# One subtraction of token_sums is issued on GpSimd in place of VectorE

## The chip, the cores and the metric

The kernel runs on one core of a Trainium2 chip. The core has five engines with their own instruction queues: TensorE (PE, matrix products; its weight loads are listed as PEld), VectorE (DVE), ScalarE (ACT), GpSimd (POOL) and SyncE (SP, which here only starts transfers). Each queue runs in order, and an instruction that must wait for another engine holds up all that stands behind it in its own queue. The metric is the device time of one execution, in microseconds; less is better.

## The reference

The kernel computes one layer of a two-stream block: a mixer with recurrent heads (up to about 1075 us of the profile, and not touched here) and then a SwiGLU channel mixer with a 3x3 depthwise convolution, in float32. What the change touches is the channel mixer's up-projection of 512 tokens of width 2048 to twice 5504 columns:

```python
def conv_ffn(h, rows, cols, w_up, conv_w, conv_b, w_down):
    u = jnp.einsum('btd,df->btf', h, w_up)
    u_gate, u_val = jnp.split(u, 2, axis=-1)
    g = lax.conv_general_dilated(u_gate.reshape(b, rows, cols, D_FF), conv_w[:, :, None, :], ...)
    g = g.reshape(b, t, D_FF) + conv_b
    return jnp.einsum('btf,fd->btd', jax.nn.silu(g) * u_val, w_down)
```

## The kernel before

**Products.** Tokens lie along the free dimension, and the 2048 channels of `h2` are 16 tiles of 128 partitions, `x2[0]` to `x2[15]` (128x512 each; the profile calls them all x). Float32 accuracy comes from three products (`mm3`): both operands are split into a high part (`hi`, a cast on ACT) and a low part (`lo`, the rest, a subtraction on DVE), and high*high, high*low and low*high are accumulated. `split` is line 105 (ACT) and line 106 (DVE), every matmul is line 111.

**Groups.** The 43 blocks of hidden columns go in one group of three and ten groups of four (`QUADS`). The first group is multiplied plainly: `up_gate(0)` (tiles named ug) and then the value half (uv), each over eight pairs of channel tiles, `kp` 0 to 7. For each pair a weight tile is loaded (raw_uv, 128x768), split into hi_uv and lo_uv, and used by 18 matmuls. The weight pools for raw hold four buffers, those for hi and lo two each, so the split of pair k waits until PE is done with pair k-2.

**Products in seven.** From the second group on, a 2x2 block product is made from seven products in place of eight (`seven`, combined again by `four`). It needs sums and differences of weight quarters (`load_sums`) and of token quarters. The token part is made once, by `token_sums(j)` for j = 7 down to 0, and used by all groups from `up_gate(1)` on. A pair j has the tiles k0 = 2j and k1 = 2j+1, each with two halves of 256 tokens, written here (k0,0), (k0,1), (k1,0), (k1,1). After two biased copies on ACT (line 1217) it does:

- first subtraction: (k0,0) = (k0,1) - (k0,0)
- second subtraction: (k0,1) = (k0,1) - (k1,1), line 1219
- third subtraction: (k1,1) = (k1,1) - (k0,0)
- split of the whole of k0 into bth (ACT) and btl (DVE), 128x512
- fourth subtraction, into a tile that is free by then (`rest`), and the split of (k1,1), 128x256

The helper `sub` is line 94, so all four subtractions are DVE rows of line 94 in the profile before. `token_last` later splits `rest` into bqh and bql. Bth, btl, bqh and bql are first read when `up_gate(1)` starts.

**Order.** The code above is recorded in program order, but each engine's final order is chosen by a scheduler, which has its own idea of how long each instruction takes; `high_priority` and `issue_after` steer it. So a change in one line can move other instructions of the same queues. In the stage concerned DVE and ACT interleave four kinds of work: the splits of the weight pairs (lo_ug, lo_uv), the token sums, the taps of the 3x3 convolution of group 0 (`convolve`, line 1295, tiles cv), and the weight sums and splits of the next unit (sum_ug, lo_aug, lo_bug).

Of the kernel before, what the change touches and what calls it, by code (L numbers as in the profile page):

```python
# [15 lines left out]
ALU = mybir.AluOpType  # L16
# [67 lines left out]
def block_kernel(ctx: ExitStack, tc: tile.TileContext, a: dict, out: bass.AP):  # L84
    nc = tc.nc
    V, S, G, PE = nc.vector, nc.scalar, nc.gpsimd, nc.tensor
# [6 lines left out]
    def sub(o, x, y):  # L93
        V.tensor_tensor(out=o, in0=x, in1=y, op=ALU.subtract)  # L94
# [9 lines left out]
    def split(hi, lo, x):  # L104
        cast[0] = S.copy(hi, x).ins  # L105
        return V.tensor_tensor(out=lo, in0=x, in1=hi.bitcast(F32), op=ALU.subtract).ins  # L106
# [1085 lines left out]
    def flat(x):  # L1192
        return x.rearrange("p a b -> p (a b)")
# [12 lines left out]
    def half(k, i):  # L1206
        return x2[k][:, HW * i : HW * i + HW]

    def rest(j):

        return half(4 * (j // 2) + 2, j % 2)

    def token_sums(j):

        k0, k1 = 2 * j, 2 * j + 1
        for k in (k0, k1):
            S.activation(x2[k], x2[k], AF.Identity, bias=modc[3][:, k : k + 1])
        sub(half(k0, 0), half(k0, 1), half(k0, 0))
        sub(half(k0, 1), half(k0, 1), half(k1, 1))
        sub(half(k1, 1), half(k1, 1), half(k0, 0))  # L1220
        split(flat(bt[0][j][:, 0:2, :]), flat(bt[1][j][:, 0:2, :]), x2[k0])
        sub(rest(j), half(k1, 1), half(k1, 0))
        split(bt[0][j][:, 2, :], bt[1][j][:, 2, :], half(k1, 1))
# [130 lines left out]
    for j in reversed(range(KP)):  # L1354
        token_sums(j)
# [185 lines left out]
```

## Time and profile before

| quantity | value |
|---|---|
| median of 3 runs | 2442.56 us (2441.49 to 2443.43) |
| the profiled execution's own time | 2441.44 us |
| span in it, first to last instruction | 2439.7 us |
| mean granted TensorE clock | 0.998 |
| GpSimd busy over the span | 175.9 us (7%), 221 instructions |

The profiled execution lies 1.12 us under the median, inside the spread of the three runs; 1.74 us of its time lie outside the span. Times in rows of the profile are microseconds from the start of the span. In the rows of the timeline the first number is the start, the second the length, and what stands in brackets is idle time of that engine just before and who ended it. The stage concerned lies between 1100 and 1182 us.

### The profile page before, as it was taken

Reading aid. Unit: us, or ns where it says so; the run is one execution under the profiler, and the core shown is the slowest. Engines: PE = TensorE matmul, PEld = TensorE weight load, DVE = VectorE, ACT = ScalarE, POOL = GpSimd, SP = SyncE. Lnnn points to the kernel's source line nnn. Section 1 sums busy time; section 2 is a strip of 40 time slices with the busy share of each in tenths; the row PEclk is TensorE's granted clock in tenths of the full one; section 3 lists DMA queues with packets and bytes.
Section 4 is the critical chain, followed back from the end, with each engine's and each line's share of the span. In section 5 each row is a group of like instructions: output and inputs, shape, how many; then the busy total and the mean of one; then the engine's idle time right before and its main releaser. Section 6 shows DMA issues by size and latency. Waiting matters only on the chain.

```text
span 2439.7 us, 38673 instructions
## 1 busy us (share of the span) xinstructions
PE 2412.9 (99%) x15434; PEld 2173.7 (89%) x15434; DVE 1793.3 (74%) x2872; ACT 1005.2 (41%) x1498; POOL 175.9 (7%) x221
## 2 busy tenths in 40 slices
PE   8999999999999999999999999999999999999998
PEld 6888999899988888888898989899999999999997
DVE  6666856555456586779987887878787878787886
ACT  4225533322233232256544454445444444444445
POOL 0000000000000000000201010101011111111021
PEclk9999999999999999999999999999999999999999
DMA  9751111233455798833646464555555555546464
GB/s 388 284 173 56 46 53 44 78 121 114 137 189 191 237 321 275 287 130 109 145 132 154 116 151 123 137 134 141 136 130 139 134 143 122 146 123 154 113 185 135
DMA packets 122487, 373.67 MB, mean 153 GB/s; under 512 B 13912, under 2 KB 19010, under 8 KB 122306
## 3 DMA queue, kind: packets, MB, share of 16 engines
q1 hardware_dynamic: 95298, 318.75, 39.8%
q0 software_dynamic: 25920, 51.40, 11.7%
q8 instruction: 121, 1.98, 0.3%
q10 hardware_dynamic: 1088, 1.05, 0.1%
q14 instruction: 60, 0.49, 0.1%
HBM read 320.80 MB, written 50.34 MB: 152 GB/s over the span
## 4 chain that ended last, share of the span: by engine, by line
PE 94%; DVE 3%; DMA 1%; ACT 1%; issue 1%; SPq 0%; POOL 0%; POOLq 0%; ACTq 0%; DVEq 0%
PE a L111 19%; PE ug L111 18%; PE uv L111 18%; PE dn L111 18%; PE ga L111 7%; PE wo L111 7%; PE po L111 2%; PE ps_m L111 1%; PE sl L111 1%; PE st L111 1%; PE cst L111 1%; DMA raw_uv<-in_w_up 0%; DVE ex L94 0%; DMA xl<-in_xT 0%; DMA raw_m<-in_w_mod 0%
## 5 line engine op out<-in xcount | busy, mean ns | idle before, releaser
L111 PE MATMUL dn<-gh,lo_d 128*128 128x512 f32 x672 | 262.5, 391 | 2.3 <-DVE lo_d L106 2.3
L111 PE MATMUL dn<-gl,hi_d 128*128 128x512 f32 x672 | 261.6, 389 | 0.0
L111 PE MATMUL dn<-gh,hi_d 128*128 128x512 f32 x672 | 261.6, 389 | 0.0
L1295 DVE SCALAR_TENSOR_TENSOR cv<-pads,cwt,cv 128x512 f32<-128x512 f32 x344 | 239.2, 747 | 0.6
L1349 POOL DMA_DIRECT2D x2d<-st x160 | 140.1, 929 | 1142.0 <-ACT st L1348 1062.2
L106 DVE TENSOR_TENSOR lo_buv<-sum_uv,hi_buv 128x1024 fp32r<-128x1024 f32 x80 | 98.0, 1225 | 102.8 <-ACT hi_buv L105 102.7
L322 DVE SCALAR_TENSOR_TENSOR raw_m<-raw_m,crow 128x1024 f32<-128x1024 f32 x128 | 154.6, 1229 | 1.7 <-DMA raw_m<-in_w_mod 1.7
L111 PEld LDWEIGHTS dn<-gh,lo_d 128*128 128x128 f32 x672 | 126.1, 188 | 31.1 <-DVE lo_d L106 5.2
L111 PE MATMUL a<-hi_h,hTh 128*128 128x256 f32 x512 | 151.7, 296 | 0.5 <-ACT e L404 0.5
L111 PEld LDWEIGHTS dn<-gl,hi_d 128*128 128x128 f32 x672 | 126.2, 188 | 26.0
L111 PEld LDWEIGHTS dn<-gh,hi_d 128*128 128x128 f32 x672 | 126.2, 188 | 25.7
L111 PE MATMUL a<-lo_h,hTh 128*128 128x256 f32 x512 | 144.7, 283 | 0.0
L111 PE MATMUL a<-hi_h,hTl 128*128 128x256 f32 x512 | 144.6, 283 | 0.0
L105 ACT CAST hi_d<-raw_d 128x1024 fp32r<-128x1024 f32 x86 | 88.6, 1030 | 130.0 <-PE ug L111 70.3
L106 DVE TENSOR_TENSOR lo_d<-raw_d,hi_d 128x1024 fp32r<-128x1024 f32 x86 | 102.9, 1196 | 48.3 <-ACT hi_d L105 47.8
L111 PE MATMUL ug<-bth,hi_bug 128*128 128x256 f32 x480 | 136.8, 285 | 0.0
L111 PE MATMUL ug<-bqh,lo_aug 128*128 128x256 f32 x480 | 135.8, 283 | 0.0
L111 PE MATMUL uv<-bqh,lo_auv 128*128 128x256 f32 x480 | 135.8, 283 | 0.0
L111 PE MATMUL uv<-bth,hi_buv 128*128 128x256 f32 x480 | 135.8, 283 | 0.0
L111 PE MATMUL uv<-btl,hi_buv 128*128 128x256 f32 x480 | 135.8, 283 | 0.0
L111 PE MATMUL uv<-bth,lo_buv 128*128 128x256 f32 x480 | 135.8, 283 | 0.0
L111 PE MATMUL uv<-bql,hi_auv 128*128 128x256 f32 x480 | 135.8, 283 | 0.0
(414 smaller groups left out, 7262.7 us busy)
## 6 DMA issues: line engine op xcount, KB each, us to landing
raw_m<-in_w_mod SPq DMA_DIRECT2D x192, 512.0 KB, 5.1
raw_d<-in_w_down SPq DMA_DIRECT2D x82, 512.0 KB, 3.5
raw_ug<-in_w_up SPq DMA_DIRECT2D x80, 512.0 KB, 3.6
x2d<-st POOLq DMA_DIRECT2D x160, 256.0 KB, 5.6
raw_uv<-in_w_up SPq DMA_DIRECT2D x80, 512.0 KB, 5.4
raw_h<-in_w_heads SPq DMA_DIRECT2D x64, 512.0 KB, 3.6
raw_ga<-in_w_gates SPq DMA_DIRECT2D x32, 512.0 KB, 3.8
raw_wo<-in_w_out SPq DMA_DIRECT2D x32, 512.0 KB, 4.5
```

What stands on the lines that cost most here:

```text
L105: cast[0] = S.copy(hi, x).ins
L106: return V.tensor_tensor(out=lo, in0=x, in1=hi.bitcast(F32), op=ALU.subtract).ins
L111: ins = PE.matmul(*args, **kw)
L322: V.scalar_tensor_tensor(out=x, in0=x, scalar=1.0, in1=crow[0], op0=ALU.mult, op1=ALU.mult, accum_out=mtot[:, at : at + 1])
L1295: V.scalar_tensor_tensor(out=t3, in0=src, scalar=w, in1=t3, op0=ALU.mult, op1=ALU.add)
L1349: nc.gpsimd.dma_start(x2d[k], t, accum_op=ALU.add)
```

## The change

One line of `token_sums`: the second subtraction is issued on GpSimd (`G`) and not on VectorE. Its operands, its shape (128x256, float32, both inputs in SBUF) and its result are the same.

```diff
         sub(half(k0, 0), half(k0, 1), half(k0, 0))
-        sub(half(k0, 1), half(k0, 1), half(k1, 1))
+        G.tensor_tensor(out=half(k0, 1), in0=half(k0, 1), in1=half(k1, 1), op=ALU.subtract)
         sub(half(k1, 1), half(k1, 1), half(k0, 0))
         split(flat(bt[0][j][:, 0:2, :]), flat(bt[1][j][:, 0:2, :]), x2[k0])
```

The scheduler's result differs on DVE, ACT and POOL, and only between the first token subtraction and the first down-projection weight (lo_d_0); the rows of PE and of SP are the same. Three places follow, each a piece of the difference (- only before, + only in the change, no sign in both); x_12 is `x2[12]`, the last number is a buffer's.

DVE's queue, where the token sums of the pairs 6 and 7 (tiles 12 to 15) begin:

```order
 L94 TENSOR_TENSOR x_12_9113<-x_12_9113 128x256
 L94 TENSOR_TENSOR x_14_9117<-x_14_9117 128x256
-L94 TENSOR_TENSOR x_12_9113<-x_12_9113,x_13_9115 128x256
-L94 TENSOR_TENSOR x_14_9117<-x_14_9117,x_15_9119 128x256
+L94 TENSOR_TENSOR x_10_8810<-x_10_8810 128x256
 L94 TENSOR_TENSOR x_13_9115<-x_13_9115,x_12_9113 128x256
+L94 TENSOR_TENSOR x_15_9119<-x_15_9119,x_14_9117 128x256
 L106 TENSOR_TENSOR lo_ug_7_9473<-raw_ug_7_9470,hi_ug_7_9472 128x768
```

The second subtractions of the pairs 6 and 7 are gone from DVE; a first subtraction of pair 5 was pulled ahead, and the third subtractions of both pairs (into x_13 and x_15), which must wait for GpSimd now because it reads what they overwrite, stand ahead of the weight split lo_ug_7.

POOL's queue, between the stores of the residual stream and the first stores of the down-projection (line 1349):

```order
 L1171 DMA x2d_7894<-x_15_9119 128x512
+L1219 TENSOR_TENSOR x_12_9113<-x_12_9113,x_13_9115 128x256
+L1219 TENSOR_TENSOR x_14_9117<-x_14_9117,x_15_9119 128x256
+L1219 TENSOR_TENSOR x_10_8810<-x_10_8810,x_11_8812 128x256
+L1219 TENSOR_TENSOR x_8_8806<-x_8_8806,x_9_8808 128x256
+L1219 TENSOR_TENSOR x_6_8496<-x_6_8496,x_7_8498 128x256
+L1219 TENSOR_TENSOR x_4_8492<-x_4_8492,x_5_8494 128x256
+L1219 TENSOR_TENSOR x_2_8184<-x_2_8184,x_3_8186 128x256
+L1219 TENSOR_TENSOR x_0_8180<-x_0_8180,x_1_8182 128x256
 L1349 DMA x2d_7879<-st_0_10364 128x512
```

The eight subtractions stand there in one run; nothing else of POOL's work is passed.

DVE's queue around the weight splits lo_uv_3 and lo_uv_4:

```order
 L106 TENSOR_TENSOR bql_9222<-x_2_8184,bqh_9214 128x256
+L106 TENSOR_TENSOR lo_uv_3_9660<-raw_uv_3_9657,hi_uv_3_9659 128x768
+L106 TENSOR_TENSOR bql_9221<-x_2_8184,bqh_9213 128x256
+L1295 SCALAR_TENSOR_TENSOR cv_9799<-pads,cwt,cv_9799 128x512
+L1295 SCALAR_TENSOR_TENSOR cv_9810<-pads,cwt,cv_9810 128x512
+L1295 SCALAR_TENSOR_TENSOR cv_9799<-pads,cwt,cv_9799 128x512
 L106 TENSOR_TENSOR bql_9223<-x_6_8496,bqh_9215 128x256
+L1295 SCALAR_TENSOR_TENSOR cv_9799<-pads,cwt,cv_9799 128x512
 L106 TENSOR_TENSOR lo_uv_4_9684<-raw_uv_4_9681,hi_uv_4_9683 128x768
```

Lo_uv_3 now stands behind all token sums, and four convolution taps stand between it and lo_uv_4, where none stood before.

## The prediction, written before the change was run

> **What bounds the kernel now.** First the page's shares of busy time and the chain that ended last, then that chain in order of time for the stage of the change (start, length, what), then busy time of each engine in stretches of that stage.
>
> ```profile
> PE 2412.9 (99%) x15434; PEld 2173.7 (89%) x15434; DVE 1793.3 (74%) x2872; ACT 1005.2 (41%) x1498; POOL 175.9 (7%) x221
> PE 94%; DVE 3%; DMA 1%; ACT 1%; issue 1%; SPq 0%; POOL 0%; POOLq 0%; ACTq 0%; DVEq 0%
> ...
> 1076.76 32.95 PE ug L111 x144
> 1109.71 32.64 PE uv L111 x144
> 1142.35 40.31 PE ug L111 x336
> ...
> 1206.99 0.74 DVE cv L1295
> 1207.74 1.15 DVE lo_d L106
> ...
> core 0: us, PE busy (x) PEld busy (x) DVE busy (x) ACT busy (x) POOL busy (x), PEclk, DMA share, GB/s
> 1080.00:1109.50 29.50, 29.50 (x132) 24.43 (x131) 29.48 (x51) 26.38 (x43) 0.00 (x0) 1.00 0.30 91
> 1109.50:1142.30 32.80, 32.80 (x147) 27.15 (x146) 32.79 (x65) 20.08 (x36) 0.00 (x0) 1.00 0.43 135
> 1142.30:1182.60 40.30, 40.30 (x338) 40.30 (x337) 37.19 (x56) 17.73 (x24) 0.00 (x0) 1.00 0.26 77
> ```
>
> TensorE sets the time: it is on 94% of the chain, and from 1080 to 1182.6 it never pauses. DVE is full as well, 62.27 of 62.3 us up to 1142.3, but always a little ahead of PE; GpSimd does nothing here. Two things follow. A gain on DVE cannot shorten this stage, since PE waits for nobody in it. A loss on DVE can lengthen it, because DVE has no idle time to absorb it; what stands between is how early each weight split comes. So the question is that margin.
>
> ```profile
> 1109.55 0.39 PE L111 MATMUL uv<-bqh,hi_uv 128*128 128x512 f32 x1
> 1110.00 0.39 PE L111 MATMUL uv<-bqh,lo_uv 128*128 128x512 f32 x1
> 1116.02 0.95 DVE L106 TENSOR_TENSOR lo_uv<-raw_uv,hi_uv 128x768 fp32r<-128x768 f32 x1
> 1117.68 0.84 ACT L105 CAST hi_uv<-raw_uv 128x768 fp32r<-128x768 f32 x1 [1.13 <-PE uv L111]
> 1118.16 0.39 PE L111 MATMUL uv<-bqh,lo_uv 128*128 128x512 f32 x1
> 1124.26 0.95 DVE L106 TENSOR_TENSOR lo_uv<-raw_uv,hi_uv 128x768 fp32r<-128x768 f32 x1
> 1126.32 0.39 PE L111 MATMUL uv<-bqh,lo_uv 128*128 128x512 f32 x1
> ```
>
> The value unit of group 0 starts at 1109.55, and eight weight pairs share its 32.64 us: 4.08 us each. A pair's low part is first read 0.45 us in (1110.00 against 1109.55). The third pair's low part is done at 1116.97 and read at 1118.16, 1.2 us later; the fifth's at 1125.21 and 1126.32, 1.1 us. It cannot be made much earlier, since only two buffers exist: at 1117.68 ACT's cast of the fourth pair had waited 1.13 us for PE to leave a buffer. **The margin is 1.1 us**, and PE can't catch up on what it loses.
>
> **The change part by part.** *What leaves DVE.* Sixteen subtractions with two named inputs are in the stage, of which eight go:
>
> ```profile
> L94 DVE TENSOR_TENSOR x<-x,x 128x256 f32<-128x256 f32 x16 | 6.0, 419 | 0.0
> 1100.76 0.76 DVE L94 TENSOR_TENSOR x<-x 128x256 f32<-128x256 f32 x2
> 1101.43 1.09 DVE L94 TENSOR_TENSOR x<-x,x 128x256 f32<-128x256 f32 x3
> 1102.44 0.95 DVE L106 TENSOR_TENSOR lo_ug<-raw_ug,hi_ug 128x768 fp32r<-128x768 f32 x1
> 1125.46 2.08 DVE L1295 SCALAR_TENSOR_TENSOR cv<-pads,cwt,cv 128x512 f32<-128x512 f32 x3
> 1127.46 0.42 DVE L106 TENSOR_TENSOR bql<-x,bqh 128x256 fp32r<-128x256 f32 x1
> ```
>
> Instructions overlap at their ends, so what counts is start to start: two 128x256 subtractions take 0.67 us (1100.76 to 1101.43), 0.335 each, and three taps 2.00 us, 0.665 each. Eight subtractions free 8 x 0.335 = 2.7 us of DVE.
>
> *What fills it.* The scheduler refills that time ahead of the same weight splits. Counted in the two queues from the first token subtraction to lo_uv_4: before 42 instructions of 128x256, 8 of 128x512, 5 of 128x768; now 35, 8, 5 and four taps. The difference is 4 x 0.665 - 7 x 0.335 = +0.3 us. So the freed time brings lo_uv_4 no margin at all, and takes 0.3 us of it. Behind lo_uv_7 DVE is then lighter, where it had time anyway (37.19 of 40.30 us).
>
> *What is added.* Eight GpSimd subtractions, and a wait of DVE for each: the third subtraction of a pair overwrites what GpSimd reads, and stands one or two subtractions behind the one that releases GpSimd. The same operation and shape is in the tail of the profile, and a GpSimd operation beside DVE work is in the mixer:
>
> ```profile
> 2424.00 3.49 POOL L1426 TENSOR_TENSOR o<-xf,r3s 128x256 f32<-128x256 f32 x5 [32.14 <-ACT r3s L1430]
> 2423.55 0.37 ACT L1430 COPY r3s<-rb_rmsf 128x256 f32<-128x256 f32 x1 [0.44 <-DVE o L97]
> 2424.68 1.41 DVE L97 TENSOR_TENSOR o<-xf,rb_rmsf 128x256 f32<-128x256 f32 x4
> 480.18 1.21 DVE L322 SCALAR_TENSOR_TENSOR raw_m<-raw_m,crow 128x1024 f32<-128x1024 f32 x1
> 485.52 0.64 POOL L975 TENSOR_SCALAR_AFFINE_SELECT ed<-ed 128x512 f32<-128x512 f32 x1 [50.83 <-ACT ed L971]
> 485.74 0.96 DVE L97 TENSOR_TENSOR qs<-qs,qk 128x512 f32<-128x512 f32 x1 [4.33 <-ACT qs L972]
> 488.52 0.64 POOL L975 TENSOR_SCALAR_AFFINE_SELECT ed<-ed 128x512 f32<-128x512 f32 x1 [2.37 <-ACT ed L971]
> 488.58 1.65 DVE L322 SCALAR_TENSOR_TENSOR raw_m<-raw_m,crow 128x1024 f32<-128x1024 f32 x1
> 490.17 0.68 DVE L97 TENSOR_TENSOR qs<-qs,qk 128x512 f32<-128x512 f32 x1
> ```
>
> One costs GpSimd 3.49/5 = 0.70 us, and it starts 0.08 us behind its releaser (2423.92 to 2424.00). Beside it DVE can slow down. At 488.58 a DVE instruction took 1.65 us, where the same took 1.21 at 480.18: 0.44 us lost while GpSimd ran beside it for 0.58 us. At 485.74, 0.96 against 0.68: 0.28 lost in 0.42. So DVE loses about 0.7 of the time that both run, and GpSimd nothing (0.64 in both). Both DVE instructions have two inputs in SBUF. In the tail, where one input (rb_rmsf) lies in PSUM, four take 1.41 us, 0.35 each as usual. Token subtractions, low parts and taps all have two inputs in SBUF, so they are the first kind.
>
> *The price D of one GpSimd subtraction to DVE.* From below, with no slowing, only the waits count: the pairs 6 and 7 give GpSimd a run of three. DVE's first goes from 1100.76 to 1101.18; GpSimd runs to 1101.96 and 1102.66; the third subtractions would have started at 1101.77 and 1102.1 and start behind those two ends, so DVE is 0.6 to 0.7 us late after a run of three: D = 0.25. With the slowing, the three take 2.1 us, about 1.75 of them beside a busy DVE, which loses 0.7 x 1.75 = 1.2 us; by then GpSimd's results are there and the waits are gone: D = 0.4. From above, DVE stands still for the whole operation and both handovers, 0.70 + 2 x 0.08: D = 0.86. I take 0.4, since the slowing is in this trace for operands of the same kind. A gain (D under zero) is excluded by the refilled queue.
>
> *Sum.* The queue brings runs of three, three and two: 1.2 + 1.2 + 0.6 (the last falls partly behind lo_uv_2) = 3.0 us; plus 0.3 for the order, less 1.1 of margin: **PE waits 2.2 us** before lo_uv_4, most of it before lo_uv_2 and lo_uv_3. With D = 0.25 it is 2.0 + 0.3 - 1.1 = 1.2; with 0.86, 6.9 + 0.3 - 1.1 = 6.1. The profiled execution would go from 2441.44 to 2443.6, the median from 2442.56 to **2444.8**.
>
> A rule of the Trainium skill speaks against the change: SBUF — State Buffer, sections Who interferes with whom and Summary: rules for kernel authors, says that a DVE instruction with two SBUF inputs contends with a GpSimd instruction that reads SBUF, and that the one issued later waits until the first is done. By that blocking in full DVE would lose 1.0 and not 0.7 of the overlap, D about 0.6, and the wait would be 3.8 us; this trace agrees that they contend, but shows 0.28 lost in 0.42 us and so not a full block.
>
> *What is hidden.* ACT's casts bth wait for GpSimd now, and behind them in ACT's queue stand hi_uv_1 to hi_uv_3; ACT is busy 20.08 of 32.80 us, and a high part is read 0.45 us before a low part that needs it first, so the low part decides. A raw tile of the next unit is fetched into the buffer that lo_uv_4 leaves, and shifts with it. Bth and bql are read from 1142.35 on, some 20 us later. GpSimd has nothing else until its stores behind 1190. Without these covers each would add its own lateness, below 1 us. PE's wait for lo_d at 1206.99 (behind a tap) lies behind a point where DVE was idle already, and is kept:
>
> ```profile
> 1178.66 1.22 DVE L106 TENSOR_TENSOR lo_d<-raw_d,hi_d 128x1024 fp32r<-128x1024 f32 x1 [1.92 <-ACT hi_d L105]
> 1208.93 0.50 PE L111 MATMUL dn<-gh,lo_d 128*128 128x512 f32 x1 [1.31 <-DVE lo_d L106]
> ```
>
> **The rivals.** *All hidden:* DVE isn't slowed, and handovers are quick enough that lateness stays within 1.1 us, 2442.6. For it: margins of over 1 us; against it: the queue's waits alone need 0.7 us per run of three and there are two runs before lo_uv_1. *Slower, beyond 0.2%:* GpSimd and DVE exclude each other, so that each of the eight holds DVE for its full 0.70 us and both handovers: 6.1 us, 2448.7, and already from D = 0.71 (5.7 + 0.3 - 1.1 = 4.9 us). For it: two inputs on GpSimd, where the rows of the mixer have one; against it: DVE kept 0.3 of its rate there. *Faster:* the relief of 2.7 us shortens a wait of PE. The nearest is that of 1.31 us before lo_d; were it to go, 2441.3. Against it: that wait's queue order is unchanged and DVE idles before it. *The change does nothing:* excluded, the eight rows are in POOL's queue.
>
> **How the numbers follow.** A difference under 0.2% (4.9 us) is about what measurements of this kernel can't tell from no change. Forecast (a wait of 0.6 to 4.9 us): 0.50. All hidden: 0.15. Slower beyond 4.9 us: 0.31, since the price of a GpSimd operation with two inputs beside a full DVE isn't in the trace. Faster than before, if only by the 1.31 us: 0.04, of which 0.03 would be beyond 0.2% by something that I don't see. Within 0.2%: 0.50 + 0.15 + 0.01 = 0.66; slower 0.31; faster 0.03. The range goes from 2441.5, the lowest run before, for the hidden case, to 2449.0, just above D = 0.86.
>
> **What would show it.** Rows of L1219 on POOL near 0.70 us each, within 1101 to 1120; DVE subtractions beside them at 0.7 to 0.85 us in place of 0.42; waits of PE before uv that name lo_uv (L106), 2 us in sum between 1113 and 1128, and none between 1143 and 1182; the wait before lo_d again at 1.3 us. GpSimd rows well over 0.70 us, or waits of PE over 4 us, would show the forecast wrong on the slow side; no wait of PE in uv, on the other.

## The result and the profile after

| | before | after |
|---|---|---|
| median of 18 runs each, side by side | 2441.85 us (2439.94 to 2444.55) | 2445.81 us (2444.68 to 2448.09) |
| ratio to before, 95% interval | | 1.0018 (1.0012 to 1.0025) |
| the profiled execution's own time, span | 2441.44, 2439.7 us | 2448.0, 2446.0 us |

The change costs 3.96 us, 0.16%: slower, since the whole interval lies above 1, but inside the 0.2% that counted as the same. The forecast was +2.2 us. That its absolute figure (2444.8) came within about 1 us of the measured median is in part luck: the median before is 0.7 us lower in this longer series than the one it started from.

The two profiled executions lie 6.6 us apart, more than the medians. Part of this has nothing to do with the change: the value unit of group 0 (uv) starts at 1112.18, where it had started at 1109.55, and ahead of it TensorE has the same work in both. (In e9 below, whose time is that of before, the unit starts at 1112.30.) One piece of these 2.6 us shows in the granted clock (the figure ahead of the DMA share) of the stretch 1073 to 1079. Before:

```profile
1073.00:1079.00 6.00, 5.56 (x38) 4.75 (x37) 5.40 (x11) 4.07 (x8) 0.00 (x0) 1.00 0.45 131
```

After:

```profile
1073.00:1079.00 6.00, 5.82 (x38) 5.52 (x38) 3.74 (x8) 2.27 (x5) 0.25 (x1) 0.72 0.54 165
```

So only stages are compared here, each from its own start. The unit's first matmul and that of the next unit, with TensorE's four waits between (timeline of PE, after):

```profile
1112.18 0.39 PE L111 MATMUL uv<-bqh,hi_uv 128*128 128x512 f32 x1
...
1117.58 0.50 PE L111 MATMUL uv<-bqh,lo_uv 128*128 128x512 f32 x1 [0.70 <-DVE lo_uv L106]
1122.94 0.50 PE L111 MATMUL uv<-bqh,lo_uv 128*128 128x512 f32 x1 [0.97 <-DVE lo_uv L106]
1127.52 0.50 PE L111 MATMUL uv<-bqh,hi_uv 128*128 128x512 f32 x1 [0.64 <-ACT hi_uv L105]
1128.80 0.50 PE L111 MATMUL uv<-bqh,lo_uv 128*128 128x512 f32 x1 [0.55 <-DVE lo_uv L106]
...
1149.03 0.28 PE L111 MATMUL ug<-bqh,hi_aug 128*128 128x256 f32 x1
```

The unit takes 1149.03 - 1112.18 = 36.85 us, where it took 32.64: **4.2 us lost here**, about the whole difference of the medians. Before, PE had no wait in the stage; now four, 2.86 us in all. The other 1.35 us stand in no wait's row, and about 1.1 of them can be found: matmuls overlap, they start 0.23 us apart while a row is 0.39 long, so a wait's row misses 0.16 us each time, and the first matmul behind a wait takes 0.50 us in place of 0.39. Some 0.3 us are left open. The waits fall on the second, third and fourth weight pair, lo_uv_1 to lo_uv_3 (without waits each pair takes 4.08 us from 1112.18 on).

What holds VectorE up is seen in the first run of three pairs (timelines of POOL and DVE, after):

```profile
1103.97 2.70 POOL L1219 TENSOR_TENSOR x<-x,x 128x256 f32<-128x256 f32 x3 [30.73 <-DVE x L94]
...
1103.41 1.09 DVE L94 TENSOR_TENSOR x<-x 128x256 f32<-128x256 f32 x3
1105.12 1.84 DVE L94 TENSOR_TENSOR x<-x,x 128x256 f32<-128x256 f32 x2 [0.63 <-POOL x L1219]
1106.88 0.95 DVE L106 TENSOR_TENSOR lo_ug<-raw_ug,hi_ug 128x768 fp32r<-128x768 f32 x1
```

Five subtractions take from 1103.41 to 1106.88, 3.47 us, where 5 x 0.335 = 1.68 would do. Three GpSimd subtractions cost VectorE 1.8 us: **0.6 each**, partly as a wait (0.63), partly as stretched instructions (1.84 us for two, where two took 0.76).

The rows of the line by itself (ns: shortest, median, longest; then who waited for it), and ACT's queue behind it, after:

```profile
L1219 POOL TENSOR_TENSOR x<-x,x x8: 726/916/1717, 1104.0 to 1123.4; 128x256 f32<-128x256 f32 x8
  ACT bth L105: 4.3, 2
  DVE x L94: 1.9, 3
...
1123.51 1.63 ACT L105 CAST bth<-x 128x512 fp32r<-128x512 f32 x3 [3.47 <-POOL x L1219]
1126.64 0.83 ACT L105 CAST hi_uv<-raw_uv 128x768 fp32r<-128x768 f32 x1
```

GpSimd pays too: 0.73 us at best, 1.72 at worst. And ACT stands 3.47 us in front of a bth cast; behind it comes the high part of the fourth weight pair, done at 1127.47, for which PE waited 0.64 us.

### The profile page after: what moved, and what is told of

Same layout as the page of the kernel before. It is cut to its first block, busy times and chain, and to the rows that moved or that the text cites. A ratio compares the mean times of both kernels' runs of the same rounds, so it can differ in the third digit from the quotient of the medians.

```text
span 2446.0 us, 38672 instructions
## 1 busy us (share of the span) xinstructions
PE 2417.0 (99%) x15434; PEld 2177.0 (89%) x15434; DVE 1793.3 (73%) x2864; ACT 1006.7 (41%) x1498; POOL 183.9 (8%) x229
## 4 chain that ended last, share of the span: by engine, by line
PE 89%; DVE 4%; issue 4%; DMA 2%; ACT 1%; POOL 0%; SPq 0%; POOLq 0%; ACTq 0%; DVEq 0%
PE a L111 19%; PE uv L111 16%; PE ug L111 16%; PE dn L111 16%; PE ga L111 7%; PE wo L111 7%; PE po L111 2%; PE ps_m L111 1%; PE sl L111 1%; DVE cv L1295 1%; PE st L111 1%; DMA raw_uv<-in_w_up 1%; PE cst L111 1%; DVE lo_d L106 0%; DVE ex L94 0%
## 5 line engine op out<-in xcount | busy, mean ns | idle before, releaser
L111 PE MATMUL ug<-bqh,hi_aug 128*128 128x256 f32 x480 | 135.8, 283 | 0.0
```

Of the source, the lines that this page charges most:

```text
L111: ins = PE.matmul(*args, **kw)
```

## The experiments

Theory A: a two-input VectorE instruction and a GpSimd subtraction never stream at the same time, so the second stream costs the first engine its length. Rival B: the third subtraction's new wait for GpSimd is the cost. Rival C: the order that the scheduler refilled is. All kernels ran beside runs of the kernel before; differences are in us against it, with the ratio's 95% interval. The last column compares the length of the uv unit in the trace, from its first matmul to the first of the next unit, with the 32.64 us of before.

| run | difference | interval of the ratio | PE's waits in the unit | unit longer by |
|---|---|---|---|---|
| the change | +4.0 | 1.0012 to 1.0025 | 2.9, four | 4.2 |
| e1, eight extra GpSimd subtractions | +5.5 | 1.0013 to 1.0030 | 2.7, one | 4.7 |
| e2, eight extra GpSimd copies | +1.2 | 0.9997 to 1.0014 | none | 0.4 |
| e3, the fourth subtraction in place of the second | +5.5 | 1.0012 to 1.0030 | 3.5, three | 4.4 |
| e4, the third into its own tile | +5.9 | 1.0014 to 1.0033 | 3.6, four | 4.9 |
| e5, VectorE's new order alone | +0.3 | 0.9995 to 1.0012 | none | 0.0 |
| e6, four pairs of eight | +2.6 | 1.0000 to 1.0018 | 0.6, two | 1.5 |
| e7, second and fourth | +9.0 | 1.0021 to 1.0045 | 4.7, four | 8.2 |
| e8, e1 with a tiny copy on VectorE | +4.3 | 1.0008 to 1.0026 | 2.2, four | 3.7 |
| e9, seven extra GpSimd memsets | 0.0 | 0.9990 to 1.0008 | none | 0.0 |
| e10, the change, taps held back | +3.8 | 1.0007 to 1.0025 | 2.8, four | 4.0 |

**e1: only GpSimd work added.** VectorE's queue is that of before, word for word.

```diff
         split(bt[0][j][:, 2, :], bt[1][j][:, 2, :], half(k1, 1))
+        lo = bt[1][j][:, 0:2, :].bitcast(F32)
+        G.tensor_tensor(out=gscr, in0=lo[:, 0, :], in1=lo[:, 1, :], op=ALU.subtract)
```

> The kernel before with all its subtractions still on VectorE, in the same order, plus eight GpSimd subtractions of 128x256 (two inputs in SBUF) into an unused tile, one behind each pair's token sums; nothing reads their result, so nothing waits for them. Theory A (a GpSimd subtraction and a VectorE instruction with two SBUF inputs stream one at a time, so each of the eight delays VectorE by about 0.6 us): seven of them lie ahead of the fifth weight pair of the uv unit, 7 x 0.6 = 4.2 us late, less the margin of 1.1 us: about +3 to +4.5 us against before, PE rows that wait for lo_uv or hi_uv between the third and the fifth weight pair. Theory A' (the price of 0.4 us in the prediction): 7 x 0.4 - 1.1 = +1.7 us. Rival B (the third subtraction's wait for GpSimd was the cost): no wait is added here, so no change, within 0.5 us. Rival C (the order of VectorE that the scheduler refilled was the cost): the order is that of before, so no change.

The loss agrees with A in kind and excludes B and C, which have nothing here to act through. In time it lies above the +3 to +4.5 expected (its interval, 3.2 to 7.3 us, reaches into them), and the waits are elsewhere than expected. GpSimd's rows by line, the second and third of them alone, VectorE beside the first, beside the second and beside the last five, and a stretch with its granted clock (e1):

```profile
L1227 POOL TENSOR_TENSOR gscr<-btl x8: 774/1058/15664, 1106.1 to 1133.0; 128x256 f32<-128x256 f32 x8
1107.95 0.77 POOL L1227 TENSOR_TENSOR gscr<-btl 128x256 f32<-128x256 f32 x1 [1.04 <-DVE btl L106]
1112.97 15.66 POOL L1227 TENSOR_TENSOR gscr<-btl 128x256 f32<-128x256 f32 x1 [4.25 <-DVE btl L106]
...
1106.24 0.96 DVE L94 TENSOR_TENSOR x<-x 128x256 f32<-128x256 f32 x1
1108.06 0.95 DVE L106 TENSOR_TENSOR btl<-x,bth 128x256 fp32r<-128x256 f32 x1
1127.94 3.54 DVE L1299 SCALAR_TENSOR_TENSOR cv<-pads,cwt,cv 128x512 f32<-128x512 f32 x3
1133.42 1.47 DVE L106 TENSOR_TENSOR lo_uv<-raw_uv,hi_uv 128x768 fp32r<-128x768 f32 x1
...
1134.00:1138.00 4.00, 3.06 (x9) 2.43 (x10) 4.00 (x8) 0.00 (x0) 0.08 (x1) 0.71 0.39 131
```

Where GpSimd gets in, VectorE pays: a subtraction of 0.96 us in place of 0.42, three taps of 3.54 in place of 2.08. But the third GpSimd subtraction is shut out for 15.66 us, through some 35 VectorE instructions that follow one another without a gap, and ends at 1128.63, 0.69 us behind the start of the first tap. Then five run in a row against the taps, the sixth weight pair is late, and PE waits 2.7 us at once. Behind that wait the granted clock was 0.71 in the mean from 1134 to 1138; nine matmuls between 1136 and 1139 start about 0.43 us apart in place of 0.23, so some 1.8 of the unit's 4.7 us are the clock's. Who is let in isn't decided by the start alone: the second GpSimd row got in with a start 0.11 us ahead of the next VectorE instruction (1107.95 against 1108.06), the third didn't with the same lead (1112.97 against 1113.08). What decides it is left open.

**e2: the same with one input.** `G.tensor_copy(gscr, bt[1][j][:, 0, :].bitcast(F32))` in the place of e1's line.

> The kernel before plus eight GpSimd copies of 128x256 (one input in SBUF) into an unused tile, at the same places as the eight subtractions of the first experiment. If every GpSimd access to SBUF excludes VectorE (theory A in its widest form), each copy costs VectorE its streaming time, between 0.3 and 0.6 us: 7 x 0.3 - 1.1 = +1 us to +3.5 us. If only a GpSimd instruction with two inputs does, or one that needs the port that VectorE's second input uses, no change, and the VectorE rows beside the copies keep 0.335 us a subtraction. Rivals B and C: no change.

GpSimd's rows and two VectorE rows beside its first (e2):

```profile
L1226 POOL COPY gscr<-btl x8: 468/740/15339, 1105.5 to 1130.1; 128x256 f32<-128x256 f32 x8
...
1104.38 0.43 DVE L94 TENSOR_TENSOR x<-x,x 128x256 f32<-128x256 f32 x1
1105.68 0.62 DVE L94 TENSOR_TENSOR x<-x 128x256 f32<-128x256 f32 x1
```

One input is enough for the exclusion (a copy was shut out for 15.34 us), but the price is 0.2 us (0.62 against 0.42) in place of 0.54. GpSimd's rows are shorter too, 0.47 us at best against 0.77; that this is the reason isn't shown. Nearly all of it stays within the margin: PE has no wait long enough for a row of its own, and the unit is 0.4 us longer. The time is unclear, its interval holds 1.

**e3 and e4: the wait of rival B taken away.** In e3 the fourth subtraction, which nothing on VectorE reads for long, goes to GpSimd. In e4 the second does, as in the change, but the third writes to a tile of its own.

```diff
-        sub(rest(j), half(k1, 1), half(k1, 0))
+        G.tensor_tensor(out=rest(j), in0=half(k1, 1), in1=half(k1, 0), op=ALU.subtract)
```

```diff
+        G.tensor_tensor(out=half(k0, 1), in0=half(k0, 1), in1=half(k1, 1), op=ALU.subtract)
+        c = gs["c"][:, HW * (j % 2) : HW * (j % 2) + HW]
-        sub(half(k1, 1), half(k1, 1), half(k0, 0))
+        sub(c, half(k1, 1), half(k0, 0))
```

> The second subtraction stays on VectorE; the fourth one (the operand of the third product) goes to GpSimd in its place, which nothing on VectorE waits for until the last splits. Theory A: the same eight GpSimd streams beside a full VectorE, the same price of 0.6 us each, so +3 to +4.5 us as the change itself. Theory A' at 0.4: about +2 us. Rival B (dependence wait): the wait is gone, so no change, within 0.5 us. Rival C (refilled order): VectorE again gives up eight subtractions and takes four taps of the convolution ahead of the fifth weight pair, so at most +0.3 us.

> The change, with the third subtraction written to a tile of its own in place of the half that the GpSimd subtraction still reads; so VectorE need not wait for GpSimd there. Theory A: the wait was only another name for the time that the streams exclude each other; most of the loss stays, +2.5 to +4.5 us against before. Rival B: the loss goes, within 0.5 us of before. Rival C: at most +0.3 us.

Both lose at least as much as the change (the unit is 4.4 and 4.9 us longer; in time both lie above the ranges expected, and their intervals reach into them): B falls, and the loss changes its bearer. In e3, GpSimd's rows and ACT's queue:

```profile
L1222 POOL TENSOR_TENSOR x<-x x8: 717/1046/9362, 1105.8 to 1126.1; 128x256 f32<-128x256 f32 x8
...
1124.79 0.41 ACT L105 CAST bqh<-x 128x256 fp32r<-128x256 f32 x1 [5.56 <-POOL x L1222]
1125.10 0.83 ACT L105 CAST hi_uv<-raw_uv 128x768 fp32r<-128x768 f32 x1
```

In e4, GpSimd's rows, and VectorE's by group (busy us, mean ns, then idle us before):

```profile
L1219 POOL TENSOR_TENSOR x<-x,x x8: 726/742/3399, 1101.9 to 1122.2; 128x256 f32<-128x256 f32 x8
...
L106 DVE TENSOR_TENSOR btl<-x,bth 128x512 fp32r<-128x512 f32 x8 | 6.1, 758 | 4.6 <-ACT bth L105 4.6
```

Without a wait VectorE runs on and shuts GpSimd out (9.36 and 3.40 us); then ACT waits 5.56 us for GpSimd with a weight pair's high part behind, or VectorE 4.6 us in all for ACT. In the change, where rival B's wait stands, no GpSimd row took over 1.72 us; so the wait seems to let GpSimd in early: a part of the price, not its cause.

**e5 and e6: the order alone, and half the dose.** e5 leaves line 1219 out, which gives VectorE the changed kernel's order, but for two first subtractions that stand two places later (the same instructions stand ahead of each weight split); e6 writes `(G if j >= 4 else V).tensor_tensor(...)` there.

> The second subtraction of each pair is left out altogether (two of the seven products are fed with a wrong operand): VectorE then has exactly the order of the changed kernel, taps of the convolution in the freed places included, with nothing on GpSimd. Theory A (the streams of GpSimd and VectorE exclude each other): no loss without GpSimd; TensorE sets the pace and VectorE has no wait to save, so no change, within 1 us, and no PE row of the uv unit that waits. Rival C (the refilled order itself is late): PE waits for lo_uv as in the changed kernel, +1 us or more. A gain of more than 1 us would show that relief on VectorE is worth something here, which the prediction denied.

> The change for the first four of the eight pairs in the order of the program (pairs 7 to 4); the other four stay on VectorE. Theory A: 4 x 0.6 = 2.4 us late by the third or fourth weight pair, of which 4 x 0.335 = 1.3 us are given back in part by the subtractions that VectorE no longer has; less the margin of 1.1 us, so 0.2 to 1.5 us of waits on PE, and +0.5 to +2 us against before: less than half of the change's loss, since the margin is paid once. If the loss went by the count alone, half of it, +2 to +2.8 us.

e5 shows no wait of PE in the unit, which takes 32.64 us as before: C falls, and relief of VectorE by 2.7 us is worth nothing here. e6's first waits come at the third pair (waits of PE by line, us in total, times, longest):

```profile
PE uv L111 <- DVE lo_uv L106: 0.4, 1, 0.4
PE uv L111 <- ACT hi_uv L105: 0.2, 1, 0.2
```

0.6 us against 2.86, a fifth of the waits for half the dose, as a margin paid once would have it. In time (+2.6, interval from nothing to +4.4) the two expectations aren't told apart. The unit's length does it: 1.5 us longer, near 4 x 0.6 - 1.1 = 1.3, where half of the change's 4.2 would be 2.1.

**e7: twice the dose.** The edits of the change and of e3 together.

> Both the second and the fourth subtraction of each pair on GpSimd: 16 in place of 8. Theory A: 16 streams of 0.6 us exclude VectorE or are kept waiting by it, and ACT's casts wait for them: about twice the loss or more, +7 to +12 us against before. If the loss came from something that happens once (a wait at one place), it stays near +4 to +6 us.

The two longest of PE's four waits and the stretch behind the first of these (e7):

```profile
1118.87 0.50 PE L111 MATMUL uv<-bqh,lo_uv 128*128 128x512 f32 x1 [1.64 <-DVE lo_uv L106]
1126.86 0.51 PE L111 MATMUL uv<-bqh,lo_uv 128*128 128x512 f32 x1 [1.91 <-DVE lo_uv L106]
...
1119.00:1123.00 4.00, 4.00 (x11) 3.14 (x12) 4.00 (x7) 2.04 (x3) 3.14 (x3) 0.57 0.37 102
```

+9.0 us, inside A's +7 to +12; a part of it is the clock of 0.57: matmuls start 0.43 us apart there for some 3 us.

**e8: a gap made for GpSimd.** e1 with `V.tensor_copy(vscr, half(k1, 1)[:, 0:1])`, one input and one column, behind each GpSimd subtraction.

> The first experiment (eight extra GpSimd subtractions whose result nothing reads) with eight tiny VectorE copies of 128x1 (one input) behind them. In the first experiment one GpSimd row took 15.7 us, which ended where VectorE came from its subtractions to the taps of the convolution. Theory A, held: VectorE keeps the access as long as one two-input instruction follows another without a gap, and gives it up at an instruction of another form. Then no GpSimd row is over 3 us here, each of eight VectorE rows is stretched by 0.6 us, and PE waits move ahead to between 1113 and 1130 us; +4 to +6 us in all. Rival D (GpSimd is kept waiting for another reason, such as the taps being the first that let it in): a row of over 10 us stays, and the time stays that of the first experiment plus 0.5 us.

GpSimd's rows, the row that was shut out for 15.66 us in e1, and VectorE where it ends (e8):

```profile
L1228 POOL TENSOR_TENSOR gscr<-btl x8: 784/830/3331, 1105.4 to 1128.0; 128x256 f32<-128x256 f32 x8
1112.21 3.27 POOL L1228 TENSOR_TENSOR gscr<-btl 128x256 f32<-128x256 f32 x1 [4.03 <-DVE btl L106]
...
1114.80 0.14 DVE L1229 COPY vscr<-x 128x1 f32<-128x1 f32 x1
1114.87 1.77 DVE L94 TENSOR_TENSOR x<-x 128x256 f32<-128x256 f32 x2
```

It now ends at 1115.48, 0.54 us behind the end of the tiny copy (1114.94). The other row of over 3 us ends likewise 0.54 us behind a tiny copy (1122.06 against 1121.52). So once GpSimd has been shut out, VectorE holds the access from one two-input instruction to the next, and lets go at the first of another form: this copy here, a tap with its per-partition scalar in e1. The longest row is 3.33 us, a little over the 3 expected, since the copies stand 2.1 to 4.9 us apart. Three of PE's four waits now lie between 1120 and 1131, 0.50 to 0.86 us each, in place of the one of 2.7.

**e9: GpSimd writes alone.** `G.memset(half(k1, 0), 0.0)` behind the token sums of seven pairs, VectorE's order as before.

> The kernel before plus seven GpSimd memsets of 128x256 (no input, writes alone) over a half that nothing reads any more, one behind the token sums of each pair but one; VectorE's order stays that of before. Theory A in the form that only reads collide (the second input of VectorE against an input of GpSimd): no GpSimd row is kept waiting (from the row of before on pads, 2.31 us for 128x2640, each about 0.3 us, none over 0.6), VectorE's subtractions keep 0.335 us each, no change, within 1 us. If writes collide too: rows of several us as in the experiments with an input, VectorE rows stretched by 0.2 to 0.3 us, and up to +1 us.

GpSimd's rows and VectorE's subtractions (e9):

```profile
L1225 POOL MEMSET x<- x7: 312/313/318, 1107.9 to 1126.2; 128x256 f32 x7
...
L94 DVE TENSOR_TENSOR x<-x,x 128x256 f32<-128x256 f32 x16 | 5.9, 417 | 0.0
```

Nothing is stretched on either side, and the time is that of before. GpSimd's writing alone doesn't collide; in e1 and e2, where it also reads, it does.

**e10: the taps held back.**

```diff
-    convs = convolve(0)
+    with tc.issue_after(late["uv0_4"]):
+        convs = convolve(0)
```

> The change, with all of the first convolution held behind the lower part of the fifth weight pair (lo_uv_4), so that VectorE does not fill the freed places ahead of it with four taps of 0.665 us. The waits of PE at the third and the fourth weight pair (0.70 and 0.97 us in the changed kernel) lie ahead of the taps and stay; those at the fifth (0.64 and 0.55 us) go, with their restart some 1.4 to 1.7 us: +2 to +2.7 us against before, where the change has +4. If the taps cost nothing, since what counts is GpSimd's streams alone, it stays at +3.5 to +4.5 us.

A miss. PE's last two waits stay as they were (e10):

```profile
1125.55 0.50 PE L111 MATMUL uv<-bqh,hi_uv 128*128 128x512 f32 x1 [0.62 <-ACT hi_uv L105]
1126.83 0.50 PE L111 MATMUL uv<-bqh,lo_uv 128*128 128x512 f32 x1 [0.55 <-DVE lo_uv L106]
...
1125.83 0.95 DVE L106 TENSOR_TENSOR lo_uv<-raw_uv,hi_uv 128x768 fp32r<-128x768 f32 x1
1128.23 2.73 DVE L1298 SCALAR_TENSOR_TENSOR cv<-pads,cwt,cv 128x512 f32<-128x512 f32 x4
```

The expectation had put these waits at the fifth pair; they are at the fourth (lo_uv from 1125.83), and the taps stand behind that in the change already. So the four taps cost nothing, as the second half of the expectation says.

## Why the prediction came out as it did

- **What bounds, and that relief is worth nothing:** right. e5 gives VectorE the relief without GpSimd, and the time stays (0.9995 to 1.0012), the unit's length to the hundredth.
- **The price D:** the term that was too small, 0.4 against 0.6 measured (1.8 us for a run of three, and see the sum below). The step that failed is "DVE loses about 0.7 of the time that both run, GpSimd nothing". The quoted affine_select rows fit full exclusion. A one-column VectorE instruction takes 0.14 us (e8), which can be taken as start-up and not stream. GpSimd's row ends at 485.52 + 0.64 = 486.16, and VectorE's at 485.74 + 0.96 = 486.70, 0.54 later: just 0.68 - 0.14, its whole stream. At 488.58 likewise: 490.23 - 489.16 = 1.07 = 1.21 - 0.14. VectorE had lost all of the overlap but its start-up. The rows of e1 bear this out with the same operands as here: VectorE's row ends 0.29 us behind GpSimd's (1109.01 against 1108.72), where 0.42 - 0.14 = 0.28. That GpSimd loses nothing was true only of those two rows, where it came first (0.73 to 1.72 us in the change). Rows well over 0.70 us were the sign that the prediction itself had named for an error on the slow side.
- **The rule of the Trainium skill** (SBUF — State Buffer, Who interferes with whom, and Summary: rules for kernel authors) was set aside with "not a full block". The price worked out by it was the right one: D 0.6, a wait of 3.8 us; the unit lost 4.2. The other half of that rule of the Trainium skill (Who interferes with whom), that a GpSimd instruction which only writes doesn't contend, agrees with e9 (313 ns, nothing stretched). The Trainium skill's "until the first finishes" (Summary: rules for kernel authors) falls short of e1, where a GpSimd row was kept out for 15.66 us, through some 35 VectorE instructions.
- **The sum:** its form was right, and e5 lets it be closed. From the unit's first matmul the fourth pair's lo_uv starts after 1120.18 - 1109.55 = 10.63 us before, after 1120.72 - 1109.88 = 10.84 in e5, and after 1127.79 - 1112.18 = 15.61 in the change. So the new order takes 0.21 us, and the eight GpSimd subtractions, VectorE's waits for them included, 4.77, which is 0.60 each. Less the margin that makes 4.98 - 1.1 = 3.9 us, and 4.2 were measured; 0.3 us stay open. The forecast 0.3 us for the order up to lo_uv_4 is there in e5 as well (15.02 us against 14.71), but the last wait lies one pair ahead of it, where 0.2 counts. The rows: the unit's first matmul, lo_uv_3 and lo_uv_4 in e5, then lo_uv_3 before, then after:

```profile
1109.88 0.39 PE L111 MATMUL uv<-bqh,hi_uv 128*128 128x512 f32 x1
1120.72 0.96 DVE L106 TENSOR_TENSOR lo_uv<-raw_uv,hi_uv 128x768 fp32r<-128x768 f32 x1
1124.90 0.97 DVE L106 TENSOR_TENSOR lo_uv<-raw_uv,hi_uv 128x768 fp32r<-128x768 f32 x1
...
1120.18 0.95 DVE L106 TENSOR_TENSOR lo_uv<-raw_uv,hi_uv 128x768 fp32r<-128x768 f32 x1
...
1127.79 0.95 DVE L106 TENSOR_TENSOR lo_uv<-raw_uv,hi_uv 128x768 fp32r<-128x768 f32 x1
```

- **Where it shows:** most of the waits were to come before lo_uv_2 and lo_uv_3, and 2.16 of the 2.86 us do (lo_uv_2, hi_uv_3, lo_uv_3). The first 0.70 us come one pair earlier than forecast, at lo_uv_1, and none comes at lo_uv_4. So the four taps stand behind the last wait, and e10 gains nothing by moving them.
- **"So the low part decides":** wrong at one pair. The fourth pair's high part stood behind a cast that waited 3.47 us for GpSimd, and PE waited 0.64 us for it.
- **The rival slower beyond 0.2%** had the mechanism, exclusion, but priced it with handovers that aren't paid in full: 6.1 us against 4.2. *All hidden* falls (PE's waits), *faster* too (e5).
- **lo_d:** to be kept at 1.3 us; its longest wait is now 0.8 (PE's waits by line, after). That this comes from the change isn't shown: in e9, whose time is that of before, it is 0.94. A later wait of 0.55 us for lo_buv (1236.24 in the trace after), which the trace before doesn't have, costs about as much as was spared.

```profile
PE dn L111 <- DVE lo_d L106: 0.9, 2, 0.8
```

No version here beats the kernel before, and the runs point to none: the stage has no wait to save, and each way of giving GpSimd a subtraction cost 3.8 us or more when all eight moved.

## What to carry to other kernels

GpSimd was no free second vector engine beside a VectorE that is full of instructions with two SBUF inputs: each GpSimd subtraction took 0.6 us from VectorE to spare it 0.335. If the overlap must be, look for who is let in: a VectorE that never pauses can shut GpSimd out (for 15.66 us in e1), and then the readers of GpSimd's result, and what stands behind them in their queues, are late. To see whether two engines share or exclude, compare the ends of two overlapping rows and take off the start-up; a lost share of the overlap misleads when the overlap is short.

## What was not expected of the hardware

- VectorE can keep the access to SBUF across instructions: one GpSimd subtraction, 0.77 us at best in that run, took 15.66 us (e1), a copy 15.34 (e2). A VectorE copy of one column ended it (e8).
- The price went with what GpSimd reads, not with its running: two inputs 0.54 us per 128x256 (e1), one input 0.2 (e2), none 0 (e9).
- After some of TensorE's longer waits the granted clock fell for some microseconds: 0.71 behind one of 2.7 us (e1), 0.57 behind one of 1.64 (e7). Behind a wait of 1.91 us in e7 it stayed at 1.00 from 1127 to 1131. Which waits bring it is left open. That last stretch (e7; the figure ahead of the DMA share is the clock):

```profile
1127.00:1131.00 4.00, 4.00 (x18) 3.16 (x18) 3.81 (x8) 2.63 (x6) 1.12 (x1) 1.00 0.38 98
```
